# New durations in the rough clock that orders the mixers' and the projection's instruction streams

## Chip, core and metric

The kernel runs on one core of one Trainium2 chip. The metric is the device time in microseconds of one execution; the median of several runs is compared. Traces come from the hardware profiler, one execution each, and count from that execution's first instruction.

Names of engines: PE is the tensor engine (PEld its weight loads), DVE the vector engine, ACT the scalar engine, POOL the GpSimd engine, SP the engine that issues most DMA transfers.

## The reference

One layer of a hybrid decoder, on 1024 prompt tokens and 8 x 4 sample tokens (1056 in all), width 1024, everything in float32:

```python
h = x + 0.5 * rms_norm(swiglu(rms_norm(x, ng[0]), gate0, up0, down0), ng[1])     # 1024 -> 2816 -> 1024
cols = rms_norm(h, ng[2]) @ w_in                                                  # the combined projection
c_gla, c_gmlp, c_rwkv, c_dil = split_at(cols, [GLA_COLS, GMLP_COLS, RWKV_COLS, DIL_COLS])
o_gla  = gla_mix(c_gla, ...)      # gated linear attention, chunks of 64
o_gmlp = gmlp_mix(c_gmlp, ...)    # spatial gating, chunks of 128
o_rwkv = rwkv_mix(c_rwkv, ...)    # RWKV-7 state update, token by token in the reference
o_dil  = dilated_mix(c_dil, ...)  # three groups of dilated windows, and caches of the sample tokens
h = h + rms_norm(concat([o_gla, o_gmlp, o_rwkv, o_dil]) @ w_out, ng[3])
y = h + 0.5 * rms_norm(swiglu(rms_norm(h, ng[4]), gate1, up1, down1), ng[5])
```

It returns y for the prompt and sample tokens, and the mixers' new states and window rows.

## The kernel before

**Products.** Every large product splits each float32 operand into a high and a low float32r part and makes three passes (`mm3`, lines L139, L142, L143; `prod`, L505 to L507, in the FFN bodies; L573, L204 and L2553 elsewhere). Tokens come in thirds of 352 columns. ACT makes the high part of a weight (L111, L476), POOL the low part (L112, L477).

**Stages.** The first half-FFN's opening and body are written out in a fixed order. From the last products of the first FFN to the first products of the second, and once more for the last products of the second, the order is made by a class `Loom`. Between lie the norm after the first FFN (`follow`: L214 adds products, L249 squares, L263 to L273 a Newton inverse root on 128x1 columns, L287 a gain, L292 the residual, L303, L311, L315, L184 the next norm's operands), the combined projection, the four mixers, the output projection, and the next norm. The second FFN's body is again fixed.

**The loom.** It holds one fill, the main line of products (`line()`: the projection's column tiles, a step being three matmuls; then the output products), and a list of live streams with priorities: the norms of the 9 token tiles, weights, RWKV pairs and their feeder, gMLP, linear attention, dilated attention and its sample part. All are Python generators. Between two yields a stream writes some instructions; the loom then reckons when their results will be there. The kernel is thus traced in the order in which a rough clock of the engines says that things become ready. `note()` runs through the instructions just written and gives each the latest of: its engine's free time, its operands' times plus a latency `LAT` of 0.14 us, and its place's release; `cost()` gives its duration. DMA transfers have formulas of their own in `note()`. A stream's next step may be written when

```python
        s[2] = now + v if isinstance(v, float) else t + MG           # step(): t is the results' time, MG = 0.1
...
            if others and self.cool() and self.weft():               # run(): PE runs thin: a step of the fill
                continue
            ok = [s for s in self.live if others and self.open(s, now)]
            go = [s for s in ok if s[2] <= now + SLACK]              # SLACK = 0.2
            if go:
                self.step(min(go, key=lambda s: s[0] - (now - s[2]) / AGE))
            elif not self.weft():
```

where `now` is PE's reckoned free time and `weft()` writes one step of the fill. So fill steps stand between a stream's steps for as long as its results are not reckoned to be there. `cool()` (L1104) is true when in the last `TICK` (3.4133 reckoned us) fewer than `WARM` = 3000 columns have passed PE, or in the last whole tick fewer than `FULL` = 3060; then a step of the fill goes first. The fill itself stops at conditions: the last column tiles wait until RWKV and gMLP are through (`L.mixed == 2`), the second half of the output projection (`"end"`, `L.mixed == 3`) until all mixers are.

**What keeps the order.** `keep()` names engines on which each instruction gets a tie to the one traced before it: DVE everywhere, POOL as well in the handoffs, in RWKV and in the last products. On the other engines and queues the traced order is the starting point, and what is ready may go ahead of what is not.

The duration formulas (`cost`, from L1078), n being the elements of a partition:

```python
            n, m = size(x.outs[0]), size(x.ins[1])                   # PE: columns, stationary columns
            if x.ins[0].dtype == F32R:
                return (max(n / 2.4, m / 1.2) + 2) / 1e3
            return (max(n, m) / 1.2 + 2) / 1e3 * (1 if x.is_transpose else 2)
        if "DVE" in e:
            return (n + 100) / 960
        if "Pool" in e:
            return (2 * n + 100) / 960
        return 0.09 + n / 1200 + 0.19 * (len(x.outs) > 1)            # ACT
```

Steps that the text speaks of: in RWKV (`unit`) the scores, an inverse of 16 x 16 blocks column by column (L1333 to L1335, 15 columns of a product and a sum on DVE, L1339 ends it, L1346 turns the result on PE), blocks of 32 (L1352 to L1357) and the state's steps (L1409 to L1415). In the dilated attention (`attend`) the scores (L1726, L1728), their bias and maximum (L1734), exp (L1743), turns (L1753) and products with the values (L1764); L2005 belongs to its sample part. The first half of the output products is L2553, with a copy on ACT (L2566); the mixers' outputs come back by L2619 and are split in L128 and L129.

Of the kernel before, what the change touches and what calls it, by code (L numbers as in the profile page):

```python
# [22 lines left out]
T = TP + TS  # L23
# [27 lines left out]
class Layer:  # L51
# [29 lines left out]
    def put(self, out, in_):  # L81
        """A store of what the scalar engine has written."""
        return self.nc.scalar.dma_start(out, in_)

# [16 lines left out]
    def parts(self, w, at=None):  # L101
        """at: a place besides the shelves: a pool for one."""
# [12 lines left out]
    def shelve(self, pools, raws, room=()):  # L115
        """The pools that the coming weights (those with n places, n times) and their raw forms take turns in."""
        self.shelves, self.turns = (pools, raws), [0, 0]
        self.room.update(room)
# [12 lines left out]
    def mm3(self, out, w, kts, m, x, cs, ncol=128, first=True, last=True):  # L131
        """out += W^T X over the given (weight row block, x tile) pairs, in three float32r passes."""
# [14 lines left out]
    def products(self, out, w, kts, m, x, cs, needs=None):  # L147
        """The same in steps. needs: the results that the i-th pair waits for."""
# [9 lines left out]
    def spread(self, st, n, by=None):  # L158
        """PSUM [128, n]: the columns' st^-1/2 on every partition, times by. Also as columns."""
# [13 lines left out]
    def factors(self, pool, ts):  # L173
        """For some thirds, on every partition."""
        r = pool.tile([128, max(1, len(ts)), TH], F32, name="R", tag="R")
        return {t: r[:, i] for i, t in enumerate(ts)}
# [10 lines left out]
    # ---- what follows products by token: tiles of 128 tokens; the last 32 tokens' rows in four parts, which lie  # L187
    # below each other ----
    def by_token(self, name, tiles, ws, kk, xs, last, y, done=None):
        """y += X^T W, as steps. ws: the four quarters of the columns; kk: pairs of a row block and an x tile;  # L190
        last: the last tokens' part of the x tiles in one piece, for float32 products."""
# [29 lines left out]
    def all_tokens(self, name, ws, kk, xs, last, y, done=None, at=None):  # L221
        """The last two tiles together, if the weights' places should come free one by one."""
# [5 lines left out]
    def gain_rows(self, g, half):  # L228
        """A gain on every partition, and as the last tokens have it."""
# [10 lines left out]
    def inverse(self, parts, i):  # L240
        """(mean of a row's squares + eps)^-1/2, from parts of the row."""
# [35 lines left out]
    def follow(self, y, i, name, res, out, hn=None, nxt=None):  # L277
        """The stream after a tile's products y: h = residual + gain * norm(y), in place. hn: a place for a tile. nxt:
        (xs, gain) of the norm that follows."""
# [43 lines left out]
    def rows(self, v, d, i, load, cs=slice(0, D)):  # L323
        """A tile from or to its rows in DRAM: d[0]; the last tokens' in d[1]."""
# [21 lines left out]
class Ffn:  # L346
    """SwiGLU; the columns of the tokens on the free axis, the results' rows. fac: the factors still to be applied to
    some thirds of xs. The hidden activations come in pairs of blocks; a pair's products with
    the last two thirds of the tokens are those of 2 x 2 block matrices (the weights' halves in both directions, the
    halves of the features by the two thirds) and take seven block products instead of eight (Strassen-Winograd).  # L350
    slots: the places of a pair of hidden blocks, of the last pair, and of the sums of halves of xs."""
# [16 lines left out]
    def gu(self, ft, t, needs=None):  # L368
        """Products in steps; the rest as a stream of its own."""
# [42 lines left out]
    def head(self, name):  # L412
        """The first two blocks by thirds, as steps of a loom's fill."""
# [21 lines left out]
    def sums(self):  # L435
        """Sums of halves of xs. With B the halves of the features (rows) by the last two thirds (columns): T1 = B12 -
        B11 in place of B12, T2 = B22 - T1, T3 = B22 - B12, T4 = B21 - T2."""
# [22 lines left out]
    def blocks(self, w, c):  # L460
        """The weights' parts A = [[k, k'], [k, k']] (rows: the two column blocks of the pair): the halves and sums
        S1 = A21 + A22, S2 = S1 - A11, S3 = A11 - A21, S4 = A12 - S2."""
# [37 lines left out]
    def prod(self, out, a, x, first=False):  # L500
        """out += A x, in three float32r passes."""
# [7 lines left out]
    def seven(self, c, j, sil):  # L509
        """A pair's gates (j = 0; returned) or hidden activations."""  # L510
# [6 lines left out]
        def done(r, t, p, v):  # L517
            """The block r of the pair's third t is in p; v: where it may go."""
# [47 lines left out]
    def down(self, fts, first, ws, raws, i, h):  # L566
        """A pair's products with half of the columns, into y's rows of a token tile."""
# [16 lines left out]
    def body(self):  # L584
        """From the first pair's products into y to the last pair's hidden activations."""
# [17 lines left out]
    def tail(self, name, done=None):  # L603
        """The last two pairs' products into y."""
# [4 lines left out]
class Residual:  # L609
    """The residual's rows, some tiles ahead."""  # L610
# [7 lines left out]
    def load(self, i=None):  # L618
        """The next tile, in the place of the i-th."""
# [11 lines left out]
class Pace:  # L631
    """Traces streams between the steps of the main line of products: a stream yields how many
    microseconds of products should come before it goes on."""
# [27 lines left out]
CW = 0.6065306597126334  # exp(-1/2)  # L661
# [12 lines left out]
def rsqrt_steps(L, pool, x, shape, tag="rsq"):  # L674
    """x^-1/2 of a few columns: an integer first guess, then Newton steps to float32's accuracy."""
# [382 lines left out]
class Loom:  # L1058
# [19 lines left out]
    def cost(self, x):  # L1078
# [9 lines left out]
        if "DVE" in e:  # L1088
            return (n + 100) / 960
# [1731 lines left out]
```

## Time and profile before

| | |
|---|---|
| device time, median of 3 runs | 2575.34 us (2561.6 to 2582.16) |
| profiled execution, span from first to last instruction | 2556.4 us (its time outside the span is not given) |
| mean granted PE clock | 0.975 |
| PE busy | 2477.5 us, 97% of the span |
| DVE, ACT, POOL busy | 1372.8, 894.4, 895.3 us |
| DMA | 217.54 MB, mean 85 GB/s |

Busy time is the union of an engine's instructions. A row of a group of instructions gives the line in the kernel, the engine, the operation, output and inputs by their names, the shape (partitions x elements), the count, then the busy time, the mean ns of one, and the idle time of the engine before them with what ended it. The granted clock is the share of full speed that PE's throttle allows in a stretch. Matmuls are pipelined in the trace, so one matmul's duration overlaps with the next one's; a gap between two starts is the better price.

### The profile page before, as it was taken

How to read it: one execution, taken by the hardware profiler on the slowest of the kernel's cores; microseconds unless marked ns; L12 is line 12 of the kernel's file. 1: busy time of each engine (PE TensorE's matmuls, PEld its weight loads, DVE VectorE, ACT ScalarE, POOL GpSimd, SP SyncE). 2: the span in 40 equal slices, each digit the busy share in tenths (PEclk: the TensorE clock that was granted, in tenths of full speed). 3: DMA queues.
4: the chain of work that ended last, by engine and by line, in shares of the span. 5: the costliest groups of instructions: out<-in, count | busy, mean ns of one | idle time of the engine just before them, and what ended most of it. 6: DMA issues, size and time to landing. Idle time of an engine off the chain costs nothing.

```text
span 2556.4 us, 40103 instructions
## 1 busy us (share of the span) xinstructions
PE 2477.5 (97%) x15735; PEld 2266.8 (89%) x15735; DVE 1372.8 (54%) x3133; ACT 894.4 (35%) x2011; POOL 895.3 (35%) x698
## 2 busy tenths in 40 slices
PE   8999999999989999999999999997999999999997
PEld 8899999999989998888878999867989999999997
DVE  6555555554476056765533657427654455444547
ACT  5433223223345242233225334325542222222331
POOL 4544444444543233231111112114254443334454
PEclk9999999999999999999988889999999999999998
DMA  4111111111144332232235657244111111111123
GB/s 118 50 44 48 50 43 50 50 50 50 52 135 129 97 109 85 80 93 64 64 111 169 186 173 227 75 148 156 50 50 50 50 50 50 50 51 49 43 75 130
DMA packets 212738, 217.54 MB, mean 85 GB/s; under 512 B 26619, under 2 KB 188052, under 8 KB 212550
## 3 DMA queue, kind: packets, MB, share of 16 engines
q1 hardware_dynamic: 181954, 188.89, 24.7%
q10 hardware_dynamic: 30596, 26.10, 3.1%
q8 instruction: 123, 2.02, 0.3%
q14 instruction: 65, 0.53, 0.1%
HBM read 171.47 MB, written 43.37 MB: 84 GB/s over the span
## 4 chain that ended last, share of the span: by engine, by line
PE 55%; DVE 10%; ACT 2%; DMA 2%; issue 1%; POOL 0%; SPq 0%; DVEq 0%; ACTq 0%; POOLq 0%
PE pd L573 7%; PE p L507 6%; PE p L505 6%; PE p L506 6%; PE pw L139 5%; PE pw L142 4%; PE pw L143 4%; PE pz L2553 2%; PE pm L1726 2%; PE po L1764 1%; PE pm L2005 1%; PE pt L204 1%; DVE rq L271 1%; DVE work L1334 1%; DVE rq L273 1%
## 5 line engine op out<-in xcount | busy, mean ns | idle before, releaser
L477 POOL TENSOR_TENSOR wlo<-wraw,whi 128x512 fp32r<-128x512 f32 x280 | 375.1, 1360 | 511.5 <-ACT whi L476 511.4
L112 POOL TENSOR_TENSOR wlo<-wraw,whi 128x1024 fp32r<-128x1024 f32 x97 | 232.8, 2400 | 570.6 <-ACT whi L111 570.0
L505 PE MATMUL p<-xh,whi 128*128 128x352 f32 x1280 | 415.8, 325 | 6.3 <-ACT y L579 6.3
L507 PE MATMUL p<-xh,wlo 128*128 128x352 f32 x1280 | 415.3, 324 | 0.0
L506 PE MATMUL p<-xl,whi 128*128 128x352 f32 x1280 | 414.0, 323 | 0.0
L139 PE MATMUL pw<-xh,whi 128*128 128x352 f32 x888 | 312.2, 352 | 1.8 <-ACT stg L2438 0.9
L476 ACT CAST whi<-wraw 128x512 fp32r<-128x512 f32 x280 | 164.8, 620 | 400.3 <-DMA wraw<-in_w_ff_gate_dram 149.7
L142 PE MATMUL pw<-xl,whi 128*128 128x352 f32 x888 | 295.5, 333 | 0.0
L143 PE MATMUL pw<-xh,wlo 128*128 128x352 f32 x888 | 294.2, 331 | 0.0
L505 PEld LDWEIGHTS p<-xh,whi 128*128 128x128 f32 x1280 | 242.5, 189 | 7.8 <-ACT y L579 7.1
L506 PEld LDWEIGHTS p<-xl,whi 128*128 128x128 f32 x1280 | 242.4, 189 | 0.7
L507 PEld LDWEIGHTS p<-xh,wlo 128*128 128x128 f32 x1280 | 241.7, 189 | 0.0
L579 DVE TENSOR_TENSOR y<-y,pd 128x512 f32<-128x512 f32 (+1 forms) x272 | 176.3, 667 | 94.0 <-PE pd L573 87.8
L573 PE MATMUL pd<-whi,hid 128*128 128x512 f32 x576 | 185.9, 399 | 0.5 <-ACT y L579 0.5
L573 PE MATMUL pd<-whi,hida 128*128 128x512 f32 x576 | 183.9, 395 | 1.3 <-ACT y L579 1.3
L139 PEld LDWEIGHTS pw<-xh,whi 128*128 128x128 f32 x888 | 172.6, 194 | 13.3 <-issue 7.6
L142 PEld LDWEIGHTS pw<-xl,whi 128*128 128x128 f32 x888 | 173.0, 195 | 2.5 <-issue 1.6
L143 PEld LDWEIGHTS pw<-xh,wlo 128*128 128x128 f32 x888 | 172.2, 194 | 1.4 <-issue 0.9
L111 ACT CAST whi<-wraw 128x1024 fp32r<-128x1024 f32 x97 | 101.9, 1050 | 162.9 <-PE p L506 67.2
L506 PE MATMUL p<-hid,whi 128*128 128x352 f32 x480 | 154.9, 323 | 0.0
L573 PEld LDWEIGHTS pd<-whi,hida 128*128 128x128 f32 x576 | 109.1, 189 | 28.8 <-issue 2.5
L573 PEld LDWEIGHTS pd<-whi,hid 128*128 128x128 f32 x576 | 109.2, 190 | 28.5 <-issue 2.5
(600 smaller groups left out, 5079.1 us busy)
## 6 DMA issues: line engine op xcount, KB each, us to landing
wraw<-in_w_ff_gate_dram SPq DMA_DIRECT2D x44, 512.0 KB
wraw<-in_w_ff_up_dram SPq DMA_DIRECT2D x44, 512.0 KB
wraw<-in_w_ff_down_dram SPq DMA_DIRECT2D x44, 512.0 KB
wraw<-in_w_in_dram SPq DMA_DIRECT2D x37, 512.0 KB
cv<-in_cache_win_dram SPq DMA_DIRECT2D x36, 256.0 KB
ck<-in_cache_win_dram SPq DMA_DIRECT2D x32, 256.0 KB
qb<-dil_q SPq DMA_DIRECT2D x32, 256.0 KB
rw_d<-stg ACTq DMA_DIRECT2D x24, 176.0 KB
```

Of the source, the lines that this page charges most:

```text
L111: nc.scalar.copy(hi, raw)
L112: nc.gpsimd.tensor_tensor(lo, raw, hi.bitcast(F32), op=OP.subtract)
L139: ins = nc.tensor.matmul(out, a, xh[:, cs], start=(first and i == 0), stop=False)
L142: nc.tensor.matmul(out, a, xl[:, cs], start=False, stop=False)
L143: nc.tensor.matmul(out, b, xh[:, cs], start=False, stop=(last and i == n - 1))
L476: nc.scalar.copy(t[0][:, i], v)
L477: nc.gpsimd.tensor_tensor(t[1][:, i], v, t[0][:, i].bitcast(F32), op=OP.subtract)
L505: nc.tensor.matmul(out, ah, xh, start=first and k == 0, stop=False, skip_group_check=True)
L506: nc.tensor.matmul(out, ah, xl, start=False, stop=False, skip_group_check=True)
L507: nc.tensor.matmul(out, al, xh, start=False, stop=k == KH - 1, skip_group_check=True)
L573: nc.tensor.matmul(p, self.hid[ft][a][:, cs], ws[h][b][:, u], start=u == a == b == 0, stop=u == a == 1, skip_group_check=True)
L579: nc.scalar.copy(y, p) if first else nc.vector.tensor_add(y, y, p)
```

## The change

Four formulas of `Loom.cost` get other constants. Nothing else that is executed differs: the instructions, tiles, transfers, priorities, latencies and conditions are the same. (Docstrings and comments are taken out, each leaving an empty line, so line numbers agree.)

```diff
             if x.ins[0].dtype == F32R:
-                return (max(n / 2.4, m / 1.2) + 2) / 1e3
+                return max(n / 2.25 + 4, m / 1.2 + 2) / 1e3
             return (max(n, m) / 1.2 + 2) / 1e3 * (1 if x.is_transpose else 2)
         if "DVE" in e:
-            return (n + 100) / 960
+            return (n + 150) / 960
         if "Pool" in e:
-            return (2 * n + 100) / 960
-        return 0.09 + n / 1200 + 0.19 * (len(x.outs) > 1)
+            return (2.1 * n + 200) / 960
+        return 0.155 + n / 1150 + 0.19 * (len(x.outs) > 1)
```

The formulas of float32 matmuls and transposes, of DMA transfers, the latency and the margins stay. The first FFN's opening has a pacing of its own that does not use these formulas.

More of the change, by code (lines that the diff above doesn't have):

```diff
@@ L1085, in cost @@
             if x.ins[0].dtype == F32R:
-                return (max(n / 2.4, m / 1.2) + 2) / 1e3
+                return (max(n / 2.25 + 4, m / 1.2 + 2)) / 1e3
             return (max(n, m) / 1.2 + 2) / 1e3 * (1 if x.is_transpose else 2)
         if "DVE" in e:
-            return (n + 100) / 960
+            return (n + 150) / 960
         if "Pool" in e:
-            return (2 * n + 100) / 960
-        return 0.09 + n / 1200 + 0.19 * (len(x.outs) > 1)
+            return (2.1 * n + 200) / 960
+        return 0.155 + n / 1150 + 0.19 * (len(x.outs) > 1)
     def clocked(self, x, t, c):
```

## The prediction

> **What bounds the kernel now.** I read the page from the top: the span, the busy time of each engine, then the 40 slices.
>
> ```profile
> span 2556.4 us, 40103 instructions
> PE 2477.5 (97%) x15735; PEld 2266.8 (89%) x15735; DVE 1372.8 (54%) x3133; ACT 894.4 (35%) x2011; POOL 895.3 (35%) x698
> ...
> PE   8999999999989999999999999997999999999997
> PEclk9999999999999999999988889999999999999998
> ```
>
> PE is busy 97% of the span and no other engine above 54%, so the kernel ends when PE has done its work. Two things make PE's work longer than it has to be: stretches without a matmul (the 7s in the PE row) and stretches at a lower granted clock (the 8s in the PEclk row). The rough clock is used only between the end of the first half-FFN and the beginning of the second, and in the last products. So I cut the span at the borders of these stages (columns: the stretch, its length, busy us of PE, PEld, DVE, ACT and POOL with instruction counts, granted clock, DMA share, GB/s).
>
> ```profile
> core 0: us, PE busy (x) PEld busy (x) DVE busy (x) ACT busy (x) POOL busy (x), PEclk, DMA share, GB/s
> 0.00:708.00 708.00, 694.45 (x3999) 645.82 (x4000) 373.51 (x552) 244.11 (x472) 316.91 (x232) 0.99 0.19 56
> 708.00:800.00 92.00, 80.87 (x624) 76.87 (x622) 80.62 (x257) 51.50 (x132) 39.03 (x24) 0.93 0.43 138
> 800.00:1320.00 520.00, 505.34 (x3612) 459.42 (x3613) 270.16 (x856) 157.84 (x359) 133.00 (x153) 0.98 0.29 83
> 1320.00:1575.00 255.00, 250.55 (x1605) 226.62 (x1603) 131.25 (x441) 101.48 (x291) 39.30 (x38) 0.90 0.63 189
> 1575.00:1740.00 165.00, 160.39 (x1123) 123.19 (x1124) 62.33 (x202) 58.38 (x161) 28.49 (x25) 0.98 0.44 135
> 1740.00:1880.00 140.00, 123.88 (x824) 114.79 (x823) 106.95 (x320) 80.02 (x192) 57.27 (x38) 0.95 0.26 84
> 1880.00:2488.00 608.00, 608.00 (x3504) 568.35 (x3503) 294.91 (x385) 186.94 (x367) 252.76 (x172) 1.00 0.17 50
> 2488.00:2557.00 69.00, 54.01 (x455) 51.79 (x453) 53.10 (x124) 14.13 (x38) 28.49 (x19) 0.90 0.38 134
> ```
>
> The two bodies of the FFNs, 0 to 708 and 1880 to 2488, are written in a fixed order that the rough clock never touches: 1316 us are out of reach. In the other 1241 us the reader should take two numbers from each row. Length minus PE busy is PE's idle time: 11.1, 14.7, 4.5, 4.6, 16.1 and 15.0 us, together 66. Length times (1 minus clock) is what the lowered clock took if the stretch is PE's: 6.4, 10.4, 25.5, 3.3, 7.0 and 6.9 us, together 59.5. So even a perfect order could win no more than about 125 us, 4.9% of the span. Everything else in those stages is matmuls that have to run in any order.
>
> **What the change does, by its own formulas.** It adds, removes and resizes no instruction and no DMA. It changes four formulas in the method that reckons a duration, and with them the moment at which each mixer step counts as ready, so the order in which steps of the mixers and steps of the projection (the fill) are written. First, are the new durations truer? Groups by line and shape (busy us, mean ns of one):
>
> ```profile
> L579 DVE TENSOR_TENSOR y<-y,pd 128x512 f32<-128x512 f32 x256 | 169.6, 682 | 88.1 <-PE pd L573 87.8
> L529 DVE TENSOR_TENSOR tmp<-p,tmp 128x352 f32<-128x352 f32 x40 | 20.9, 523 | 111.9 <-PE p L507 111.9
> L271 DVE SCALAR_TENSOR_TENSOR rq<-rq 128x1 f32<-128x1 f32 x135 | 47.9, 366 | 1.7
> L1334 DVE TENSOR_TENSOR work<-B,work 128x16 f32<-128x16 f32 x8 | 4.5, 561 | 0.3
> L111 ACT CAST whi<-wraw 128x1024 fp32r<-128x1024 f32 x97 | 101.9, 1050 | 162.9 <-PE p L506 67.2 <-PE pw L142 64.3 <-DMA wraw<-in_w_ff_gate_dram 7.0
> L538 ACT COPY tmp<-p 128x352 f32<-128x352 f32 x80 | 36.0, 450 | 63.8 <-PE p L507 63.8
> L112 POOL TENSOR_TENSOR wlo<-wraw,whi 128x1024 fp32r<-128x1024 f32 x97 | 232.8, 2400 | 570.6 <-ACT whi L111 570.0 <-POOL wlo L112 0.6
> ```
>
> DVE: 512 elements, old 637 ns, new 690, trace 682; 352 elements, old 471, new 523, trace 523. ACT: 1024 elements, old 943, new 1045, trace 1050; 352 elements, old 383, new 461, trace 450. POOL: 1024 elements, old 2238, new 2448, trace 2400. DVE's narrow operations stay far off: 128x1 goes from 105 to 157 where the trace has 366, and 128x16 from 121 to 173 where it has 561.
>
> PE's matmuls overlap in the trace, so their duration is no price. What counts is the step from start to start: a run of the chain (start, us, what) and two rows of the order of time, which are the first and the last of 26 matmuls in a row.
>
> ```profile
> 1917.77 5.55 PE pd L573 x24
> ...
> 1924.32 16.86 PE pd L573 x72
> ```
>
> ```profile
> 1329.80 0.32 PE L142 MATMUL pw<-xl,whi 128*128 128x352 f32 x1
> ...
> 1333.78 0.33 PE L143 MATMUL pw<-xh,wlo 128*128 128x352 f32 x1
> ```
>
> 512 columns take 5.55 / 24 = 0.231 us and 16.86 / 72 = 0.234; the new formula has 0.232, the old 0.215. 352 columns take 3.98 / 25 = 0.159; new 0.160, old 0.149. So PE's new term is right too, and a fill step of three 352-column matmuls is reckoned at 0.481 us in place of 0.446, 7.9% more. Here a rule speaks against the change: the Trainium skill, page "TensorE: Matmul & The Clock Gate", section "Back-to-back issue gap", gives N/2.4 + 2.5 ns for a lone matmul at full clock and about 131 ns sustained at 512 columns. By it the old formula was right or still too slow, and the new PE term would put too little fill between the steps. This trace disagrees, with 231 and 234 ns at 512 columns.
>
> **How far the order can move.** A mixer step counts as ready when its results do; until then fill steps are written. Between the matmuls of a typical RWKV step and the next stand a latency of 0.14, one DVE operation on 512 elements, and a margin of 0.1, less a slack of 0.2. That is 0.677 us by the old formulas and 0.730 by the new, or 1.52 fill steps before and 1.52 after: two steps either way. After an ACT copy of 512 elements it is 0.557 / 0.446 = 1.25 and 0.640 / 0.481 = 1.33, two either way; after an ACT copy of 256 elements 0.77 and 0.87, one either way. Both sides of the ratio grow alike. So for most steps the same amount of fill stands between the same steps, and the change works at the margins: steps made of many narrow DVE operations, and the rule that calls for fill when PE runs thin.
>
> **The sum.** First the stage of the RWKV mixer, 800 to 1320. PE's waits there (total, times, longest):
>
> ```profile
> PE pm L1346 <- DVE TT L1339: 5.5, 4, 1.8
> PE pm L1352 <- ACT work L1347: 2.8, 3, 1.2
> ```
>
> The first one is the loop over 15 columns of two narrow DVE operations each (L1334, L1335). It grows by 30 x 0.052 = 1.6 us in the rough clock; the four waits are 5.5 / 4 = 1.4 us on average. Fill should then cover them: I take -5, between 0 and -14.7, all idle time of the stage. If the cover fails, because the column loop is reckoned at a third of its real 561 ns even now, the wait stays and nothing is lost.
>
> Next, the thin stretch of attention and linear attention, 1320 to 1575. Its middle, and the fill in it (first row all engines, then the rows of L139, one per fill step, by stage):
>
> ```profile
> 1400.00:1500.00 100.00, 100.00 (x585) 90.48 (x584) 54.86 (x175) 39.84 (x133) 13.58 (x14) 0.81 0.60 180
> ...
> 800.00:1320.00 520.00, 220.44 (x639) 0.98 0.29 83
> 1320.00:1575.00 255.00, 78.26 (x212) 0.90 0.63 189
> ```
>
> PE has no idle moment from 1400 to 1500 and still runs at 0.81: it is the thinness of the small matmuls that costs the clock, 25.5 us in the stage. The kernel's own rule asks for fill when fewer than 3000 columns have passed in 3.41 reckoned us. At the old price that is 37% of the tick in fill, at the new price 40%, so the rule fires about 8% sooner. 8% of 212 steps are 17 steps, 8 us of fill drawn into the stage. How much clock that buys, no row shows; the ends are 0 and -25.5. I take a quarter, -6, nearer to 0, because 212 steps in 255 us were not enough and 8% more is little. The Trainium skill, same page, section "Why this matters for your kernels", ties a drop of the clock to idle gaps over about 3 us. By that rule no drop could stand in a stretch without a gap and more fill could not mend it; the sum would be -5. The trace speaks against it, with 0.81 at 100.00 busy.
>
> The handoffs (708 to 800, 1740 to 1880, 2488 to the end) are chains of the norms on DVE, whose 80.6 us of 92 leave little to reorder. Their waits on PE, first of 708 to 800, then of 1745 to 1890:
>
> ```profile
> PE ptx L311 <- ACT hn L303: 10.9, 3, 5.8
> ...
> PE ptx L311 <- ACT hn L303: 11.4, 4, 5.8
> ```
>
> One 5.8 us wait less or more in each is the range, 12 us both ways; I take 0. The end of the mixers, 1575 to 1740, I also take at 0, with the price of its failure below. DMA issues on SP's queue move with the streams that hold them; their reckoning is unchanged, and I take 0.
>
> Sum: -5 - 6 = -11 us, span 2556.4 to about 2545. The profile gives no time around the span; the median of the runs shown, 2575.3, is 18.9 above it, and I carry that over: **2564 us**. The three runs differ by 20 us, so under 1% (25.8 us) a measurement of this kernel tells little from no change.
>
> **Rivals.** (1) It does little: the order is tied down only on DVE, and on POOL in some stages, and the amount of fill between steps keeps its whole number. Then only noise moves: 2575. For it: 15 us of waiting in 520. Against it: the narrow DVE steps do move. (2) Slower, the fill runs dry. The 1575 to 1740 stage lives on the first output products:
>
> ```profile
> 1575.00:1740.00 165.00, 67.84 (x432) 0.98 0.44 135
> ...
> 1723.22 6.17 DMA mx<-mix_d
> 1729.40 4.98 DMA wraw<-in_w_out_dram
> ```
>
> Already now the chain goes through two loads of together 11.2 us when the fill is through. If the mixers' streams grow in the rough clock by more than the fill's 7.9% (the narrow DVE operations grow by 50%), fill is used up earlier. Each fill step drawn forward leaves 0.48 us uncovered at the end, at half clock as much again. The 17 steps above and as many more from narrow steps are 34 x 0.48 = 16 us idle and up to 16 us of clock: 2575 + 32 - 5 = 2602. It decides from about 25 steps on (24 us). For it: the fill is finite and ends with the mixers. Against it: ACT and DVE grow like the fill in the ratios above, and the later fill waits for conditions of the mixers. (3) Clearly faster: the clock of 1320 to 1575 comes back nearly whole (-25), with the RWKV waits (-8) and one wait in each handoff (-6): 2536. For it: the rows show the price; against it: 8% more fill.
>
> **Chances.** Forecast 0.42, little 0.23, clearly faster 0.20, slower 0.15. The first two lie within 1% (2549.6 to 2601.1), the third is faster, the fourth mostly over the edge: faster 0.20, same 0.65, slower 0.15. The range takes in both outer rivals with their spread: 2532 to 2604.
>
> **What would show it.** Right: the waits of L1346 on L1339 fall from 5.5 towards 0; the granted clock of the attention stage rises above 0.90 with more than 212 fill steps in it; the fixed bodies keep their 708 and 608 us; PE's idle time before the output products' second half stays near 5 us. Wrong: the stage after the attention loses clock or gets longer by more than 10 us, a handoff gains a wait of 5 us, or many matmuls wait on DVE because its fixed order now puts a late operation ahead of a ready one; then that wait leads the list.

## The result, and the profile after

The changed kernel takes **2600.19 us** (median of 4 runs, 2599.17 to 2601.83) against 2568.47 for the kernel before beside it (4 runs, 2559.62 to 2582.16): ratio 1.0127, 95% interval 1.0099 to 1.0156. It is slower by 1.3%, 36 us above the forecast of 2564. Rival 2 gave 2602, which is near; how far it was right is told further below. One slow execution of the kernel a_jit below (2892 us, mean granted clock 0.777) is left out of all comparisons.

From the page of the kernel after: span and counts, busy time, then the PE and clock rows of the 40 slices.

```profile
span 2598.7 us, 40096 instructions
PE 2505.0 (96%) x15735; PEld 2291.2 (88%) x15735; DVE 1361.4 (52%) x3133; ACT 895.8 (34%) x2011; POOL 891.5 (34%) x698
...
PE   8999999999989999999999999987999999999997
PEclk9999999999999999999989869698999999999998
```

The same 15735 matmuls take 42.3 us longer in this pair of traces. The first trace of before is one of its quicker executions: the median spans are 2562.3 us over 102 recorded executions of before (2549.4 to 2576.5) and 2598.2 us over 4 of after, 36 us apart. The clock row has its low slices, 8, 8, 6, 6 and 8 among 9s, between 1300 and 1819 us (a slice is 65.0 us); before had four 8s side by side, from 1278 to 1534. Next the stages of after, cut at the same points of the work (columns as in the prediction's table).

```profile
core 0: us, PE busy (x) PEld busy (x) DVE busy (x) ACT busy (x) POOL busy (x), PEclk, DMA share, GB/s
0.00:708.00 708.00, 694.14 (x4004) 645.66 (x4005) 374.98 (x552) 244.03 (x472) 318.23 (x232) 1.00 0.18 56
708.00:800.00 92.00, 82.56 (x638) 79.58 (x637) 78.58 (x263) 52.41 (x133) 36.35 (x24) 0.93 0.44 143
800.00:1352.00 552.00, 542.51 (x3810) 496.23 (x3808) 265.16 (x853) 162.82 (x366) 139.24 (x156) 0.97 0.29 83
1352.00:1500.00 148.00, 138.92 (x862) 126.68 (x860) 60.78 (x221) 64.86 (x177) 21.86 (x20) 0.93 0.63 191
1500.00:1694.00 194.00, 187.48 (x1233) 168.64 (x1233) 86.87 (x292) 67.93 (x208) 20.52 (x22) 0.78 0.43 127
1694.00:1767.00 73.00, 57.52 (x294) 25.75 (x293) 31.70 (x111) 17.31 (x49) 11.14 (x15) 0.90 0.48 145
1767.00:1925.00 158.00, 142.29 (x966) 131.05 (x965) 115.85 (x336) 85.82 (x204) 61.75 (x41) 0.96 0.30 98
1925.00:2531.00 606.00, 606.00 (x3491) 566.30 (x3490) 294.45 (x387) 186.47 (x366) 253.03 (x172) 1.00 0.16 50
2531.00:2599.00 68.00, 53.56 (x452) 51.34 (x450) 53.02 (x123) 14.14 (x38) 29.39 (x19) 0.90 0.40 136
```

And the part from RWKV's end to the second half of the output products as one row, first of before, then of after; then the rows of the fill's two kinds in it (L139, one per projection step; L2553, the first output products), in the order before, after.

```profile
1320.00:1722.00 402.00, 395.44 (x2602) 334.80 (x2601) 189.57 (x631) 155.35 (x444) 61.29 (x58) 0.93 0.55 166
```

```profile
1352.00:1767.00 415.00, 383.92 (x2387) 321.07 (x2386) 179.35 (x623) 150.09 (x432) 53.53 (x56) 0.85 0.51 153
```

```profile
1320.00:1722.00 402.00, 79.75 (x215) 0.93 0.55 166
...
1575.00:1722.00 147.00, 67.84 (x432) 0.98 0.41 126
```

```profile
800.00:1352.00 552.00, 244.99 (x706) 0.97 0.29 83
1352.00:1767.00 415.00, 52.49 (x144) 0.85 0.51 153
...
1500.00:1694.00 194.00, 74.98 (x432) 0.78 0.43 127
1694.00:1767.00 73.00, 0.00 (x0) 0.90 0.48 145
```

Read them together. Both fixed bodies (708; 608 and 606), the opening handoff (92, 92), the one behind the output (158, where before's 1722 to 1880 is also 158) and the end (69, 68) kept their length. The change is between 800 and 1767: RWKV's stage grew from 520 to 552 us, the rest from 402 to 415, 45 in all.

- RWKV's stage: 67 more projection steps (639 to 706). At the 0.48 us of the prediction they are 32 us, all of its growth. This is work moved, not lost. Its idle time fell from 14.7 to 9.5 us, but length times (1 minus clock) rose from 520 x 0.02 = 10.4 to 552 x 0.03 = 16.6, so nothing was won there.
- The rest had 71 steps fewer (215 to 144), 34 us of work less, and yet became 13 us longer. PE's idle time rose from 402 - 395.44 = 6.6 to 415 - 383.92 = 31.1 us, and length times (1 minus clock) from 28.1 to 62.3. Together they rose by 59 us where 47 are missing; they overlap where PE was idle at a lowered clock.
- Where: the projection is used up at 1500 instead of about 1575. The 432 matmuls of L2553 then lie in 194 us at 0.78; before had them in 147 us at 0.98. They too are through when the mixers are not: from 1694 to 1767 no fill is left, and 15.5 of the 73 us are idle. (The mixers' last product of L2005 ends at 1756.)

The waits of PE, after, first of 800 to 1350, then of 1352 to 1767 (total, times, longest):

```profile
PE pm L1346 <- DVE TT L1339: 3.0, 3, 2.0
PE pm L2360 <- POOL mvn L2350: 2.0, 1, 2.0
...
PE pm L2005 <- DMA cv<-in_cache_win_dram: 5.1, 10, 0.9
PE pm L1863 <- DVE rst L682: 3.8, 1, 3.8
PE po L1764 <- ACT on L1767: 3.4, 1, 3.4
```

And PE's first wait in each of the two handoffs, 708 to 800 and 1767 to 1925:

```profile
PE ptx L311 <- ACT hn L303: 9.4, 3, 4.7
...
PE ptx L311 <- ACT hn L303: 8.1, 2, 6.5
```

The wait that the prediction wanted gone went from 5.5 to 3.0. The second stretch's list is new: the chain of attention's last products (L1764, L1863, L2005), which before hid behind L2553.

### The profile page after: what moved, and what is told of

It reads as the page before. It is cut to its first block, busy times and chain, and to the rows that moved or that the text cites. A ratio compares the mean times of both kernels' runs of the same rounds, so it can differ in the third digit from the quotient of the medians.

```text
span 2598.7 us, 40096 instructions
## 1 busy us (share of the span) xinstructions
PE 2505.0 (96%) x15735; PEld 2291.2 (88%) x15735; DVE 1361.4 (52%) x3133; ACT 895.8 (34%) x2011; POOL 891.5 (34%) x698
## 5 line engine op out<-in xcount | busy, mean ns | idle before, releaser
L505 PE MATMUL p<-xh,whi 128*128 128x352 f32 x1280 | 414.4, 324 | 6.3 <-ACT y L579 6.3
L139 PE MATMUL pw<-xh,whi 128*128 128x352 f32 x888 | 311.1, 350 | 1.7 <-ACT stg L2438 0.9
L505 PEld LDWEIGHTS p<-xh,whi 128*128 128x128 f32 x1280 | 241.3, 189 | 7.8 <-ACT y L579 7.1
L139 PEld LDWEIGHTS pw<-xh,whi 128*128 128x128 f32 x888 | 171.9, 194 | 11.7 <-issue 6.9
```

Source lines behind the costliest of these rows:

```text
L139: ins = nc.tensor.matmul(out, a, xh[:, cs], start=(first and i == 0), stop=False)
L505: nc.tensor.matmul(out, ah, xh, start=first and k == 0, stop=False, skip_group_check=True)
```

## The experiments

The rival theories, by the letters that the expectations use. **A**: the new durations draw the fill forward, so that the end of the mixers is bare. **B**: DVE's fixed order puts late operations ahead of ready ones. **C**: PE's new price moves the rule that calls for fill when PE runs thin. After the first runs A became **E**: what is lost is clock and idle time where the mixers lack fill, so putting the fill back puts the time back. **F**: any other order is somewhere between as good and 1.3% worse than the one before, and how much is that order's luck. **G**: the truer durations make a worse order by what they reckon. All ratios are to the kernel before, run in turns on the same chip (its medians were 2562.8 to 2568.5); they are taken over all runs of a kernel and are not the quotients of the medians.

Counts of my own stand in the table. From the one trace of each kernel: projection steps ahead of attention's first product (L1726); and, from the end of RWKV's last product (L971) to the first product of the second FFN (L505), PE's idle time and length times (1 minus clock), called lost clock. From all recorded executions of a kernel (102 of before, 4 to 12 of the others): the median of span times (1 minus clock), the lost clock of the whole.

| kernel | steps ahead of attention | idle | lost clock | lost clock, whole, median | median us | ratio, 95% |
|---|---|---|---|---|---|---|
| before, two traces | 808 | 25, 25 | 34, 49 | 69 | | 1 |
| after | 880 | 46 | 67 | 100 | 2600.2 | 1.0127, 1.0099 to 1.0156 |
| early | 890 | 50 | 58 | 81 | 2580.7 | 1.0061, 1.0042 to 1.0080 |
| late | 807 | 27 | 65 | 76 | 2569.1 | 1.0029, 1.0004 to 1.0054 |
| only_dve | 897 | 44 | 70 | 85 | 2573.7 | 1.0031, 1.0012 to 1.0050 |
| only_pe | 784 | 28 | 56 | 95 | 2592.1 | 1.0106, 1.0060 to 1.0152 |
| only_act | 852 | 32 | 60 | 85 | 2592.5 | 1.0108, 1.0064 to 1.0151 |
| no_dve | 842 | 23 | 55 | 80 | 2576.2 | 1.0036, 1.0019 to 1.0053 |
| gate5 | 856 | 40 | 49 | 81 | 2578.3 | 1.0034, 1.0008 to 1.0059 |
| gate6 | 800 | 29 | 65 | 105 | 2594.2 | 1.0109, 1.0085 to 1.0133 |
| heat2 | 880 | 38 | 72 | 99 | 2607.2 | 1.0157, 1.0114 to 1.0199 |
| pe_w35 | 825 | 28 | 56 | 77 | 2576.1 | 1.0038, 1.0020 to 1.0057 |
| b_w32 | 821 | 35 | 46 | 69 | 2574.3 | 1.0043, 1.0025 to 1.0060 |
| blat20 | 890 | 37 | 53 | 74 | 2566.1 | 1.0012, 0.9990 to 1.0035 |
| lat08 | 830 | 25 | 53 | 80 | 2568.4 | 1.0011, 0.9985 to 1.0038 |
| a_jit | 864 | 44 | 56 | 88 | 2585.2 | 1.0073, 1.0050 to 1.0095 |
| b_jit | 810 | 33 | 44 | 69 | 2567.7 | 1.0013, 0.9997 to 1.0030 |
| early_g5 | 856 | 42 | 72 | 104 | 2595.4 | 1.0122, 1.0101 to 1.0144 |
| latA20_g4 | 856 | 43 | 69 | 93 | 2588.5 | 1.0089, 1.0068 to 1.0110 |

### Which half of the time, which formula

**early** uses the new durations until RWKV and gMLP are through and the old ones from there on; **late** is the reverse.

```diff
             gm = ...
-            L.mixed = 2
+            L.mixed, loom.NEW = 2, not loom.NEW     # early starts with NEW = True, late with False
```

> All four new formulas until RWKV and gMLP are through, the old ones from there on. Theory A (fill drawn forward: the new durations make the RWKV stage take more fill steps than it needs, and attention and the sample streams later run without): in the written order 890 fill steps stand before the attention's first scores (L1726), against 808 before the change and 880 with it; so the loss is that of the change, 2595 to 2610 us, and the fill is through by about 1510 us of the trace. Rival B (the new order on the tied engine DVE is itself worse, wherever the new durations hold): about half of the loss, 2580 to 2590. Rival C (the loss is made after RWKV, by the new order of attention and its clock): the time of the kernel before, 2560 to 2575.

> The old formulas until RWKV and gMLP are through, the four new ones from there on. Theory A: 807 fill steps before L1726, as before the change (808), so the time of the kernel before, 2560 to 2575. Rival B: about half of the loss, 2580 to 2590. Rival C: the whole loss, 2595 to 2605.

Early costs 0.61%, late 0.29%: half of the loss comes with the durations in RWKV's stage, though it is paid behind it (50 us idle and 58 of lost clock against 25 and 34 to 49), a quarter with those of the rest. Early was cheaper than A had said and just inside B's range, late came out as A had it, and C missed both. The one traced execution of late lay 15 us above its median, so its row in the table counts for little.

**only_dve, only_pe, only_act** take one formula alone; **no_dve** takes the three others.

```diff
-            return (n + 100) / 960
+            return (n + 150) / 960                               # only_dve
-                return (max(n / 2.4, m / 1.2) + 2) / 1e3
+                return max(n / 2.25 + 4, m / 1.2 + 2) / 1e3      # only_pe
-        return 0.09 + n / 1200 + 0.19 * (len(x.outs) > 1)
+        return 0.155 + n / 1150 + 0.19 * (len(x.outs) > 1)       # only_act
```

> Only DVE's formula new (n + 150). Theory A: RWKV's chains are made of DVE operations, each 0.052 us dearer in the rough clock while a fill step keeps its old price, so the fill runs ahead most here: 897 fill steps before L1726 (808 before, 880 with the whole change); 2600 to 2625 us. Rival B: a change of DVE's order alone, as bad as the whole, 2590 to 2605. Rival C (the clock rule, moved by PE's price): PE's price is old, so about the time before, 2560 to 2575.

> Only PE's formula new (n / 2.25 + 4). Theory A: the fill grows dearer and the mixers do not, so less fill is drawn forward: 784 fill steps before L1726 (808 before); 2550 to 2572 us, the attention stage at a higher clock than 0.90. Rival B: some of the loss, as any new order, 2575 to 2590. Rival C: the whole loss, 2595 to 2605.

> Only ACT's formula new. 852 fill steps before L1726, 28 of the mixers' matmuls after the last L2553. Theory E: between the kernel before and the changed one, 2570 to 2588. Theory F: 2570 to 2582, no more than the others. If only PE's term costs: 2560 to 2572.

> The changed formulas of PE, ACT and POOL, DVE's old. 842 fill steps before L1726 (808 before, 880 changed), 54 matmuls of L2553 after the last of L2005. Theory E: fill lasts to the end as before the change, 2565 to 2582. If PE's formula costs by itself whatever the fill (it measured 2592 alone): 2588 to 2605. Theory F: between, 2580 to 2600.

The rows of L139 from 772 to 1300 show what each formula does to the fill, in five kernels, one row each: before, after, only_dve, only_pe, only_act.

```profile
772.00:1300.00 528.00, 223.78 (x649) 0.98 0.30 87
```

```profile
772.00:1300.00 528.00, 239.68 (x698) 0.98 0.31 89
```

```profile
772.00:1300.00 528.00, 239.58 (x704) 0.99 0.31 91
```

```profile
772.00:1300.00 528.00, 220.16 (x636) 0.97 0.30 87
```

```profile
772.00:1300.00 528.00, 231.02 (x675) 0.99 0.31 90
```

DVE's longer durations draw the fill forward (+55 in this stretch, +89 steps up to attention), ACT's too (+26, +44), PE's longer fill steps hold it back (-13, -24). That is shown. But the time does not follow it: only_dve draws forward most, with 897 steps, and costs 0.31%; only_pe draws none, with 784, and costs 1.06%. A and B are both wrong about only_dve and A about only_pe; C was right on only_dve and 3 us too high on only_pe; only_act lies above what any theory gave, and no_dve came out as E had it. And the parts do not add up: DVE 0.31%, PE 1.06% and ACT 1.08% alone, 1.27% all together, 0.36% without DVE. POOL's formula was not run alone.

Only_pe also tests what the prediction hoped for in the attention. The rows of L139 from attention's first product to the mixers' end, before and only_pe:

```profile
1349.00:1722.00 373.00, 66.78 (x176) 0.92 0.54 161
```

```profile
1336.00:1748.00 412.00, 78.58 (x200) 0.88 0.51 156
```

24 more fill steps stand there, and the clock is not higher: 0.88 against 0.92, and 0.89 in before's second trace.

### Putting the fill back

**gate5** and **gate6** are the kernel after, with the fill's last stretch waiting for RWKV's and gMLP's end from further ahead. **early_g5** is early with gate5's line.

```diff
-            if i == m - 1:
+            if i == m - 5:      # gate5; m - 6 in gate6
                 yield lambda: L.mixed == 2
```

> The changed kernel; the fill waits for RWKV's end four column tiles earlier (the condition on L.mixed == 2 at the fifth tile from the last three, in place of the first). Durations and the RWKV order up to there are those of the change. In the written order the output products outlast the mixers again (39 matmuls of L2553 after the last of L2005, 33 before the change; with the change none, and 100 matmuls of the mixers after the last L2553). Theory E (the time goes to windows of low PE clock where the mixers are left without fill; what counts is how the fill lasts): much of the loss comes back, 2570 to 2586. Theory F (the new order itself, on DVE or anywhere, costs, however the fill lasts): 2592 to 2610.

> The kernel after, but the fill's last stretch waits for RWKV's and gMLP's end from six column tiles before the last instead of one: 800 fill steps before attention's first product (before 808, after 880), and 26 products of the second fill behind the mixers (before 33; after leaves 100 mixer matmuls uncovered). The distribution of the fill is that of the kernel before, the fine order that of the new durations. Theory E (what is lost is the fill drawn forward): the loss goes whole, 2558 to 2572. Theory F or G (the fine order costs by itself, whether by luck or by the durations): 2574 to 2598, with 50 us or more of the time from RWKV's end to the output products at half clock, where before has 29.

> The new durations until RWKV and gMLP are through, the old ones from there on (as in early), and the fill's last stretch waits for RWKV's end from five column tiles before the last instead of one (as in gate5): 856 fill steps before attention's first product (early 890), 37 products of the second fill left behind the mixers (early 58 mixer matmuls left uncovered). Theory E: the loss of early (+0.6%) goes: 2560 to 2572. Theory F: one more order, 2565 to 2595, no relation to early. Theory G: as early, 2576 to 2586, because the reckoning is the same.

Gate5 took three quarters of the loss away, as E had it. Gate6, with 800 steps ahead of attention nearer still to before's 808, gave nearly all of it back (as F had it), and early_g5 lost twice what early had lost. Gate6 from attention's first product to the output products, then just behind RWKV, then inside attention.

```profile
1355.00:1757.00 402.00, 394.87 (x2487) 332.84 (x2486) 176.53 (x609) 148.96 (x433) 53.38 (x53) 0.87 0.52 154
1320.00:1400.00 80.00, 61.20 (x310) 52.28 (x311) 20.56 (x90) 33.28 (x79) 7.63 (x7) 0.75 0.53 161
1400.00:1500.00 100.00, 100.00 (x605) 88.62 (x603) 55.73 (x183) 35.18 (x110) 16.39 (x17) 0.83 0.62 184
```

Held back to the count of before, the fill is missing just behind RWKV (0.75 from 1320 to 1400, with 18.8 us idle), and the following stage loses its clock all the same: 402 x 0.13 = 52 us. The expectation called that the old distribution; it is so only in the count at attention's start, for between RWKV's end and attention's first product gate6 has 16 steps (1320 to 1355) where before has 46 (1315 to 1349). E does not hold as a rule for the time. Early_g5 was missed by all three theories, by F by under 1 us.

### The clock itself

**heat2** is the kernel after, with pairs of bfloat16 matmuls on 352 columns whose results nobody uses, written when the rule finds PE thin and no fill can be had (106 in all).

```diff
-            if others and self.cool() and self.weft():
-                continue
+            if others and self.cool():
+                if self.weft():
+                    continue
+                if self.heat and sum(n for _, n in self.flow) < 2400:
+                    self.heat()
```

> The changed kernel with 106 useless bfloat16 matmuls of 352 columns (results never read) written where its own rule finds PE thin and no fill is to be had, nearly all after the last output product. At the 0.16 us of a 352-column step they are 17 us of added PE work. Theory E: they keep the clock up while the mixers finish alone, and cost little or win, 2585 to 2602. Theory F, or if the stretch is bound by waits and not by the clock: added work is added time, 2605 to 2620.

```profile
1500.00:1694.00 194.00, 184.51 (x1219) 166.64 (x1219) 88.56 (x286) 66.38 (x200) 20.95 (x22) 0.78 0.47 136
1694.00:1767.00 73.00, 71.06 (x434) 35.82 (x433) 28.66 (x100) 16.84 (x49) 9.24 (x11) 0.98 0.43 127
```

They all landed from 1701 on and raised the bare end from 0.90 to 0.98, with PE busy 71.06 of 73 us. No time came of it; the kernel was, if anything, slower, inside the range of F. From the last L2553 to the last L2005 it took 74 us in place of 62. So the higher clock did not pay for the added work there; as the useless matmuls pass the same engine as the mixers' own, the run does not tell what the clock alone is worth. From 1500 to 1694, where the 0.78 is, none landed: there the rough clock still had fill, or did not find PE thin enough (under 2400 columns).

**pe_w35** raises the rule's two limits for only_pe's price; **b_w32** does so for the kernel before.

```diff
-WARM = 3000
+WARM = 3500                    # pe_w35, with PE's new formula; 3250 in b_w32, old formulas
-TICK, FULL = 3.4133, 3060
+TICK, FULL = 3.4133, 3500      # 3300 in b_w32
```

> Only PE's formula new, and the rule that calls for fill set to 3500 columns instead of 3000 and 3060. PE's formula alone measured 2592 with fill left over at the end (93 matmuls of L2553 after the last of L2005) and 46 us lost to the clock in attention. Now 825 fill steps stand before L1726 (784 without the new threshold, 808 before the change) and none of L2553 after the last L2005. Theory E: attention gets the fill that was left over, 2562 to 2580. Theory F: another order, no reason for a gain, 2585 to 2600.

> The kernel before; only the rule that calls for fill asks for 3250 columns instead of 3000 and 3300 instead of 3060. 821 fill steps before L1726 (808), 1 matmul of L2553 after the last L2005 (33): fill spread a little more and used to the end. Theory E: 2555 to 2570, and less lost to the clock in attention. Theory F: some loss as for any other order, 2572 to 2582.

The higher limits make up 16 us of only_pe's loss (E was right) and cost the kernel before 0.43% (F was right). So more fill in thin places is not a gain by itself; whether the limit has to fit the price, as C would have it, one run on each side does not show. `FULL` also does a second thing: after a tick under it the rough clock doubles PE's durations (`clocked`, L1096), so both edits change the reckoning too.

### Other reckonings

**blat20** is before with a latency of 0.20 us; **lat08** is after with 0.08. **a_jit** and **b_jit** are after and before with 0.145, a change of 5 ns. **latA20_g4** is before with 0.20 until RWKV's end, 0.14 from there on, and the gate at `m - 4`.

```diff
-LAT = 0.14
+LAT = 0.20        # blat20; 0.08 in lat08, 0.145 in a_jit and b_jit
```

> The kernel before with all its old durations; only the latency that the rough clock adds before each dependent instruction is 0.20 us instead of 0.14. That grows every chain by about what the new DVE and ACT terms add, and so draws fill forward in the same way: 890 fill steps before L1726 (808 before, 880 changed), 44 of the mixers' matmuls after the last L2553. Theory E (fill used up in RWKV, mixers left alone at low clock): slower without any new duration, 2578 to 2602. Theory F (any new order costs some, however the fill lasts): 2570 to 2580. If the truth of the durations matters: 2560 to 2575, as before.

> The changed kernel, all four new durations, with the latency at 0.08 us instead of 0.14, which takes back what the new terms add to the chains: 830 fill steps before L1726, 76 matmuls of L2553 after the last L2005. Theory E: the loss of the change goes, 2563 to 2582. If the new durations themselves cost: 2590 to 2605. Theory F: 2570 to 2580.

> The kernel after, with LAT (the latency that the rough clock adds to every operand) at 0.145 us in place of 0.14: 5 ns, far less than any duration that the change corrected, so a new order from nearly the same reckoning. Fill steps written before attention's first product: 864 (after 880, before 808); 34 mixer matmuls are left behind the last product of the second fill (after 100). Theory F (any new order falls somewhere between no loss and about 1.3%, and the size is that order's own luck): anywhere from 2563 to 2600, more than half the chance below 2590. Theory G (the truer durations themselves make the order worse, through what they reckon): within 8 us of the kernel after, 2592 to 2608. Theory E (what is lost is the fill drawn forward): between, 2580 to 2596.

> The kernel before, with LAT at 0.145 us in place of 0.14; all durations as before. Fill steps before attention's first product: 810 (before 808); 14 mixer matmuls are left behind the last product of the second fill, where before has 33 of that fill's behind the mixers. Theory F: slower than before by anything up to 1.3%, most likely 0.2 to 0.8%, 2570 to 2588, for the old constants were the best of many orders and any other order gives that up. Theory G and theory E: the same reckoning and the same distribution of fill, so no difference beyond noise, 2558 to 2573.

> The kernel before with LAT 0.20 until RWKV and gMLP are through, 0.14 from there on, and the fill's last stretch held back from four column tiles before the last: 856 fill steps before attention's first product, 4 mixer matmuls left uncovered. The longer latency alone had taken idle time and lost clock of RWKV's stage from 36 to 11 us in its profile, and lost 34 us behind it. Theory E: the gain stays and the loss goes, 2535 to 2556, faster than both kernels. Theory F: one more order, 2562 to 2595.

Blat20 from 800 to 1352 (its RWKV ends at 1346), then from attention's first product to the mixers' last:

```profile
800.00:1352.00 552.00, 547.22 (x3908) 503.92 (x3906) 265.64 (x868) 169.97 (x375) 143.21 (x160) 0.99 0.31 87
...
1372.00:1729.00 357.00, 337.78 (x2216) 284.12 (x2217) 173.92 (x604) 136.82 (x415) 48.01 (x50) 0.87 0.53 161
```

A longer reckoned latency leaves only 4.8 us idle in the first row, at 0.99, and draws the fill forward as far as early does (890 steps). It costs nothing that can be measured: 2566, where E had it slower. That is a balance. Behind RWKV it does lose, as E would have it: 19.2 us idle and 357 x 0.13 = 46 of lost clock, where before has 2.4 and 30 (rows further below). But its RWKV stage loses some 10 us, where before's loses 14.7 + 10.4 = 25. So fill drawn forward need not cost on the whole. With the new durations and a shorter latency, lat08 costs nothing either, as E had it. The case that the truth of the durations decides fits blat20 (2560 to 2575) and fails for lat08 (2590 to 2605). Then G: 5 ns on the latency took 40% of the loss from the kernel after (a_jit, 1.0073, inside the ranges of F and E; G had 2592 to 2608, the median is 2585.2). The durations alone therefore do not fix the size. On the side of before the same 5 ns cost nothing that can be measured (b_jit, 1.0013), which is below F's range and inside that of G and E. latA20_g4, by which E would have beaten both kernels, is 0.89% slower. None of these versions beats the kernel before.

**before_2** is the kernel before, unchanged, traced again.

> The kernel before once more, unchanged, for a second trace: how far the clock that is lost behind RWKV's stage varies between two executions of one program. All theories read the difference between before and after from one trace of each; if before's second trace loses over 15 us more there than its first (29 us from attention's first product to the output products), the size of that difference isn't known to better than that.

From attention's first product to the output products, first trace, second trace:

```profile
1349.00:1722.00 373.00, 370.65 (x2459) 313.04 (x2459) 182.87 (x609) 144.19 (x428) 55.62 (x53) 0.92 0.54 161
```

```profile
1354.00:1736.00 382.00, 379.30 (x2457) 320.55 (x2457) 182.42 (x608) 144.28 (x428) 55.64 (x53) 0.89 0.52 156
```

One program, with the same idle time (2.4 and 2.7 us), lost 373 x 0.08 = 30 us of clock in one execution and 382 x 0.11 = 42 in the next, and was 9 us longer there; the spans are 2556.4 and 2569.1. So a single trace tells the lost clock behind RWKV to some 15 us, and of after's +33 against before's first trace (67 to 34) 18 are left against its second.

### What is settled, and what is not

Over the 18 orders of the table (before with the mean of its traces; heat2 left out, as it has after's order), the ratio goes with the lost clock of whole executions at a correlation of 0.88, with the lost clock behind RWKV in the one trace at 0.64, and with the steps ahead of attention at 0.07. Of the 36 us between the median spans of before and after, the lost clock makes 31 (69 to 100). So what the slower orders lose is mostly clock. Fill drawn forward does leave PE idle behind RWKV (steps against idle: 0.78), but the whole time does not follow it.

None of the theories holds as the expectations put it. By their ranges E was right on six runs (no_dve, gate5, pe_w35, lat08, a_jit, b_jit) and wrong on seven; F was right on five (heat2, gate6, b_w32, a_jit, latA20_g4); G was right on gate6 and b_jit and wrong on a_jit and early_g5. What is left is a description: every order that was tried, 17 in all, measured between 1.0011 and 1.0127, and with all four new formulas and only a latency or a gate moved the ratios are 1.0011, 1.0034, 1.0073, 1.0109 and, unmoved, 1.0127. The neighbours of the old constants (1.0012, 1.0013, 1.0043, and latA20_g4 with 1.0089) spread as widely, so the runs do not show that the new durations as such make worse orders. **Open** stays why the order before is the lowest of all, and which places of the attention stage decide whether 34 or 72 us of clock are lost. No run isolated one such place.

## Why the prediction was wrong, step by step

- **The step that failed is "two steps either way".** It set one DVE operation between two RWKV steps and let the ratio 0.677/0.446 against 0.730/0.481 stand for the stage. The stage has 856 DVE operations, and at 0.052 each their reckoned time grows by 44.5 us; an estimate from that is 44.5 / 0.446 = 100 fill steps if all of it were on the chain. The DVE formula alone drew 89 more ahead of attention. All four together drew 72, where the text allowed 17 and in rival 2 "as many more". The text had a warning at hand: it reckoned itself that the column loop of L1334 and L1335 grows by 1.6 us, but used this for a wait alone. The loop runs 8 times, which makes some 28 fill steps of 0.446. This step explains where the fill went; how much time that cost it does not explain, as the 0.07 above says.
- **The attention term, -6, had the wrong sign.** It took 17 steps drawn *into* the stage, by PE's price, and a higher clock for them. From RWKV's end to the output 215 steps became 144, taken by DVE's and ACT's formulas, and the lost clock rose from 28.1 to 62.3 us. PE's price alone did put 24 more steps behind attention's first product (only_pe), and the clock there did not rise. So the link from more fill to more clock, for which the text had no row, failed too; why stays open.
- **"The end of the mixers, at 0": wrong.** Rival 2 named the mechanism and the mark, PE's idle time before the output's second half: it went from 6.6 to 31.1 us. The text's own sign of being wrong came too: the stage of the first output products went from 147 us at 0.98 to 194 at 0.78. Rival 2's price (16 idle, 16 clock, from 34 steps) was of the right kind, 25 and 34 against 71 steps. That each step drawn forward costs 0.48 us, at half clock twice that, is not what the other orders show: blat20 draws 82, loses behind RWKV, wins in its RWKV stage, and measures 1.0012. That 2602 lies so near to 2600 is partly luck: half the steps, and a base of 2575 where before beside it measured 2568.
- **RWKV's waits, -5: right in size, half by luck.** The stage's idle time fell by 5.2 us, but the wait of L1346 gave only 2.5 of its 5.5, and 6 us more of lost clock ate the gain. The 561 ns of L1334 are one shape of 15; over all 120 operations before's trace has 250.
- **Handoffs 0, fixed bodies unchanged: right.** The longest wait of L311 on L303 is 4.7 us at the first and 6.5 at the second, where it was 5.8 at both; neither handoff changed its length.
- **The new durations.** The matmul rows that made PE's new term look right are still right, at full clock; after a thin tick the rough clock doubles the price (L1096), which the text left out. A truer duration just did not make a better order.
- **The 18.9 us added to the span** are not time around it. In after's profiled execution that is 2600.65 - 2598.7 = 2.0 us; the rest is one execution of before against others.
- **The cause of the clock.** The Trainium skill, page "TensorE: Matmul & The Clock Gate", section "Why this matters for your kernels", ties a drop to PE idle for over about 3 us. Here too the trace does not agree: gate6 from 1400 to 1500 has PE busy 100.00 of 100 us, no two starts of matmuls over 0.6 us apart, and a clock of 0.83. The rule gave no help in telling the orders apart.

## What to carry to other kernels

A scheduler's constants can be judged only by the order that they happen to make: making durations truer gives another order, and here every other order was slower by 0.1 to 1.3%. Before forecasting such a change, add the new durations over the whole stage (operations times the difference) and see which finite supply is used up sooner, rather than compare one typical wait; that tells where the fill goes, not yet what it costs. And where a formula is to be judged, run its neighbours (a constant moved by 4%) beside it, for one order says little about the formula.

## What the runs showed of the hardware

The granted clock in these traces is whole or half and changes in steps of 3.413 us, and what passes PE in such a step goes with the next one's clock, with different limits in the two directions. My own count over four traces (before twice, after, gate6; 700 to 1900 us), a matmul of n columns and K rows counted as n x ceil(K/32) / 4 in the step where it starts; 7 steps without a matmul, all followed by half, are left out:

| columns in a step | full clock: followed by half | half clock: stayed half |
|---|---|---|
| under 2000 | 40 of 46 | 80 of 84 |
| 2000 to 2450 | 10 of 33 | 21 of 24 |
| 2450 to 2950 | 8 of 60 | 8 of 14 |
| 2950 and more | 0 of 1084 | 2 of 54 |

Once halved, PE has half the rate with which to come above the limit (in after, from one 352-column matmul of the projection to the next a median of 161 ns at full clock and 294 at half), so a thin stage tends to stay half: after has 35 steps that stayed, before 16 and, in its second trace, 21. The same matmuls in the same order fell on either side of the limits in two executions, which is the likeliest reason, not a tested one, for the spread of 27 us in the spans of before; how the steps' phase against the program comes about was not tried.
